# Attention: queries turned in the projection, kept turned in DRAM, and the maxima's row sent through DRAM

## The chip, the cores and the metric

The kernel runs on one core of one Trainium2 chip. The time is device microseconds of one execution, as the median of several runs; a profile is one further execution, recorded by the hardware profiler.

## The reference

One layer of a hybrid backbone. 2048 latent tokens and 256 context tokens of 1024 channels pass one input projection; latent queries (8 heads of 64, 2 key heads) read all latent and context keys in one softmax; a gated branch mixes tokens in chunks of 128; both branches are merged by gates, projected and added, and a feed-forward part with squared ReLU follows. Everything is float32.

```python
q_x = apply_rope(rmsnorm(q_heads(q_x), q_norm_g[l]), cos, sin) * q_scale
k_all = jnp.concatenate([k_c, k_x], axis=2)
v_all = jnp.concatenate([v_c, v_x], axis=2)
s = jnp.einsum('bkgqd,bknd->bkgqn', q, k)      # 2304 keys
p = jax.nn.softmax(s, axis=-1)
o = jnp.einsum('bkgqn,bknd->bkgqd', p, v)
gm_x = gmlp_spatial(gelu(u_x), gelu(vg_x), gm_norm_g[l], gm_ws[l], gm_bs[l])
x = x + g1 * branch_merge(attn_x, gm_x, ga_x, gb_x, ...)
x = x + g2 * sq_relu_mlp(modulate(x, norm2_g[l], sh2, sc2), w_ff1[l], w_ff2[l])
```

## The kernel before, in words

**Precision.** Every float32 product is made of three matmuls on a high part (rounded to the type fp32r by a copy) and a low part (the remainder that a subtraction leaves). So an operand is first *cast* on ScalarE and then its *remainder* is made on VectorE.

**Stages.** Projection and gates run from the start to about 743 us, attention from about 750 to 1430 us, then the merge and the feed-forward part. In the projection (`project`, `tick` L655) the product's matmuls (L1453 to L1455) are written in groups; pieces of side work, written as generators, are advanced by one step at each tick of that list: the query work (`queries_work` L730 to 752), the spatial mixing of the gated branch (L777 on, with its matmuls at L183 to L185 and four slots of the pool `m`), the gates. A `yield` in such a generator puts what follows at a later tick.

**Query work.** For each of 4 blocks of 512 tokens (`TB`; `TT` = 4 tiles of 128 tokens) the queries are loaded in two halves of 4 heads, normalized, turned by the rotary step (`rope` L443, its last instruction L458) and stored token by token in DRAM (`q_d` L218).

**Attention.** A `Unit` (L1850 on) is one block of 512 queries and one pair of heads: 16 units. `attend` (L1084 to L1136) goes through 18 key tiles per unit in 3 groups (gi) of `GROUP` = 6. For each tile, `first` makes the scores by the high queries (L1949) and `second` by the low ones (L1968), ScalarE takes the exponential (L1972), `values` multiplies by the values (L1982), and GpSimd and VectorE sum the probabilities (L1998, L1995, L2011). The scores need each query's maximum beforehand. While a unit runs, TensorE therefore also makes the next unit's scores once in one pass (`maxima`, L1914), which VectorE reduces from PSUM (L1920, L1925); `reference` reduces these to one number per query and head (L1931, with its sign at L1932). The low operand has 128 rows: 64 for a constant and the negative maximum, 64 for the remainder. So the subtraction of the maximum is part of the matmul.

**A unit's queries before.** `load` brings a pair's queries from DRAM, `cast` (L1874) and `remainder` (L1877) split them, `queries` turns the high part by eight transposes (L189, a helper) and two copies (L1889), and `low_queries` does the same with the remainder and the maxima. `load`, `cast` and `remainder` run two units ahead in the first group, `queries` in the second, `reference` one unit ahead in the second group, and `low_queries` at the end of the unit.

**Order.** In attention, TensorE and VectorE follow the order that the source is written in; ScalarE, GpSimd and the queues get theirs from a scheduler. The queue of SP works in order: a transfer that waits holds up the ones behind it. During the first few units VectorE and TensorE also compute part of the modulation vectors (`mod`: L364, L368, the matmuls and L381, L383).

Of the kernel before, what the change touches and what calls it, by code (L numbers as in the profile page):

```python
# [10 lines left out]
F32 = mybir.dt.float32  # L11
F32R = mybir.dt.float32r
# [39 lines left out]
def f32(ap):  # L52
    return ap.bitcast(F32)
# [17 lines left out]
class Kern:  # L71
# [119 lines left out]
    def constants(self):  # L191
# [8 lines left out]
        nc.vector.memset(self.ones, 1.0)  # L200
        self.lead = cp.tile([P, 1], F32, name="lead")
        nc.vector.memset(self.lead, 0.0)
        nc.vector.memset(self.lead[0:1], 1.0)
        self.G1 = cp.tile([P, KC, 2], F32, name="G1")
        self.S1 = cp.tile([P, KC, 2], F32, name="S1")
        self.G2 = cp.tile([P, KC], F32, name="G2")
# [8 lines left out]
        def spill(n, shape):  # L215
            return [dp.tile(shape, F32, tag=f"{n}{b}", name=f"{n}_d{b}") for b in range(NB)]

        self.q_d = spill("q", [TB, NH * HD])  # L218
        self.gm_d = spill("gm", [512, TB])
        self.at_d = spill("at", [512, TB])  # L220
        self.ta_d = spill("ta", [D, TB])
# [508 lines left out]
    def queries_work(self, b):  # L730
        nc = self.nc
        q = [self.m4([TT, 4, HD]) for _ in range(2)]
        flat = [x.rearrange("p t h d -> p t (h d)") for x in q]
        src = self.pr_d[0][b]
        nc.sync.dma_start(flat[0][:, :, :P], self.rows(src[0], slice(2 * P, 3 * P)))
        nc.sync.dma_start(flat[0][:, :, P:], self.rows(src[1], slice(0, P)))
        nc.sync.dma_start(flat[1], self.rows(src[1], slice(P, 3 * P)))
        yield
        yield
        rbs = self.heads_rstd(q, 1.0 / HD)  # L740
        yield
        tabs = self.rope_tables("q", b)
        for c, (raw, rb) in enumerate(zip(q, rbs)):
            nc.vector.tensor_tensor(out=raw, in0=raw, in1=rb, op=ALU.mult)
            yield
            qo = self.m4([TT, 4, HD])
            self.rope(tabs, raw, qo, self.m4([TT, 4, HD]), 4)
            nc.sync.dma_start(
                self.rows(self.q_d[b], slice(c * 256, (c + 1) * 256)),
                qo.rearrange("p t h d -> p t (h d)"),  # L750
            )
            yield

    def raw_values(self, b, j, c):
        x = self.m4([TT, 4, HD])
# [328 lines left out]
    def attend(self, units, late, mod):  # L1084
        self.psum({"b": 8})
        begin = self.here()
        pend = []
        for i, u in enumerate(units):
            at = lambda n: units[n] if 0 <= n < len(units) else None
            nxt, far, old, older = at(i + 1), at(i + 2), at(i - 1), at(i - 2)  # L1090
            for gi, g in enumerate(range(0, NKT, GROUP)):
                group = range(g, g + GROUP)
                step = nxt if gi < 2 else far
                for j in group:
                    u.first(j)
                    u.second(j)
                    if j % GROUP == 2 and far:
                        if gi == 0:
                            far.load()
                        elif gi == 1:  # L1100
                            far.queries()
                    if not nxt:
                        next(late, None)
                    elif i and j % GROUP == 4:
                        next(mod, None)
                if gi == 2 and nxt:
                    nxt.low_queries()
                if step:
                    step.maxima(3)
                for f in pend:  # L1110
                    f()
                if gi == 0 and far:
                    far.cast()
                if gi == 2 and old:
                    old.sums()
                if step:
                    step.maxima(3)
                if gi == 0:
                    if older:
                        older.inverse()  # L1120
                    if far:
                        far.remainder()
                if gi == 1:
                    if nxt:
                        nxt.reference()
                    if old:
                        old.join()
                pend = [lambda u=u, j=j: u.values(j) for j in group]
            pend.append(u.leave)
        for _ in mod:  # L1130
            pass
        for f in pend:
            f()
        units[-2].inverse()
        units[-1].join([self.sb("raw", [TB]) for _ in range(2)])
        self.fixed.append(range(begin, self.here()))  # L1136
# [508 lines left out]
    def build(self):  # L1645
# [27 lines left out]
        def tail(g, p):  # L1673
            u, v = units[0], units[1]
            n = KC - 2
            if (g, p) == (n + 1, 0):
# [1 line left out]
                key_load(0)  # L1678
                u.cast()
                u.remainder()  # L1680
            elif (g, p) == (n, 1):
                u.queries()
            elif (g, p) == (n + 1, 1):
                low_load(0)
            elif (g, p) == (n, 5):
# [1 line left out]
            elif g >= n and p not in (0, 1):  # L1687
                if (g, p) == (n + 1, 5):
# [1 line left out]
                    v.cast()  # L1690
                    v.remainder()
                    value_load((0, 1))
                if (g, p) == (n, 6):
                    v.queries()
                if (g, p) == (n + 1, 6):
                    key_load(1)
                    value_load((2, 3, 4))
# [3 lines left out]
                if (g, p) == (n + 1, 3):  # L1701
                    u.maxima(len(u.todo))
                    u.reference()
                    u.low_queries()
                    v.maxima(6)

        self.project(tail)
# [142 lines left out]
class Unit:  # L1850
# [8 lines left out]

    def load(self):  # L1860
        k, nc = self.k, self.nc
        self.qt = k.t2([TT, 2, HD])
        nc.sync.dma_start(
            self.qt.rearrange("p t h d -> p t (h d)"),
            k.q_d[self.b].rearrange("(t p) c -> p t c", p=P)[
                :, :, self.p * P : (self.p + 1) * P
            ],
        )
        self.pa = k.t4([TT, 2, 2, HD], F32R)
        self.pb = k.t4([TT, 2, P])  # L1870
        nc.gpsimd.memset(self.pb[:, :, :, :HD], 0.0)  # L1871

    def cast(self):
        self.nc.scalar.copy(self.pa, self.qt.unsqueeze(3).broadcast_to([P, TT, 2, 2, HD]))  # L1874

    def remainder(self):
        self.nc.vector.tensor_tensor(  # L1877
            out=self.pb[:, :, :, HD:], in0=self.qt, in1=f32(self.pa[:, :, :, 0, :]),
            op=ALU.subtract,
        )  # L1880

    def turned(self, src):
        k = self.k
        out = []
        for h in range(2):
            ps = k.bank([TB])
            k.transposes(ps, [src(t, h) for t in range(TT)])
            q = k.h2([TB], F32R)
            self.nc.scalar.copy(q, ps)  # L1889
            out.append(q)  # L1890
        return out

    def queries(self):
        self.qa = self.turned(
            lambda t, h: f32(self.pa[:, t, h]).rearrange("p a d -> p (a d)")
        )
        self.mx = self.k.small([TT, 2, NB + 1])

    def maxima(self, n):
        k, nc = self.k, self.nc  # L1900
# [26 lines left out]
                    )  # L1927

    def reference(self):
        nm = self.k.small([TT, 2])  # L1930
        self.nc.vector.tensor_reduce(out=nm, in_=self.mx, axis=AX.X, op=ALU.max)  # L1931
        self.nc.vector.tensor_scalar(  # L1932
            out=self.pb[:, :, :, 0:1], in0=nm.unsqueeze(3), scalar1=-1.0, scalar2=None,
            op0=ALU.mult,
        )

    def low_queries(self):
        self.qb = self.turned(lambda t, h: self.pb[:, t, h, :])

    def keys(self, j):  # L1940
        c, i = (0, j) if j < CTX // P else ((j - 2) // TT + 1, (j - 2) % TT)
# [148 lines left out]
```

## Time and profile before

| | us |
|---|---|
| median of 3 runs | 3111.57 (3110.06 to 3111.89) |
| the profiled execution | 3096.51 |
| its span | 3094.7 |
| TensorE busy in the span | 2991.8 (97%) |
| VectorE busy | 2062.1 (67%) |
| ScalarE busy | 1465.5 (47%) |
| GpSimd busy | 688.6 (22%) |

The profiled execution is 1.8 us longer than its span, which runs from the first to the last instruction. A row of a timeline has start, length, engine, line, operation, output and input, the number of instructions it gathers, and in brackets the idle time before them with its releaser. A row of groups has the busy time, the mean in ns, and the idle time before. PE is TensorE, PEld its weight loads, DVE VectorE, ACT ScalarE, POOL GpSimd, SP the engine whose queue issues most transfers.

### The profile page before, as it was taken

Reading aid. Unit: us, or ns where it says so; the run is one execution under the profiler, and the core shown is the slowest. Engines: PE = TensorE matmul, PEld = TensorE weight load, DVE = VectorE, ACT = ScalarE, POOL = GpSimd, SP = SyncE. Lnnn points to the kernel's source line nnn. Section 1 sums busy time; section 2 is a strip of 40 time slices with the busy share of each in tenths; the row PEclk is TensorE's granted clock in tenths of the full one; section 3 lists DMA queues with packets and bytes.
Section 4 is the critical chain, followed back from the end, with each engine's and each line's share of the span. In section 5 each row is a group of like instructions: output and inputs, shape, how many; then the busy total and the mean of one; then the engine's idle time right before and its main releaser. Section 6 shows DMA issues by size and latency. Waiting matters only on the chain.

```text
span 3094.7 us, 37963 instructions
## 1 busy us (share of the span) xinstructions
PE 2991.8 (97%) x13501; PEld 2253.6 (73%) x13501; DVE 2062.1 (67%) x2918; ACT 1465.5 (47%) x2296; POOL 688.6 (22%) x506
## 2 busy tenths in 40 slices
PE   7999999979999999999999989999999999999999
PEld 4877788866555555556877878887777788888777
DVE  4776577866887777678654488776665566654445
ACT  5646664654554545554222255444454344444433
POOL 0000000002898888885234300000000000000000
PEclk8999999989999999999999999999999999999999
DMA  8686766643110000005855459887766644445665
GB/s 298 204 264 215 233 194 202 195 151 118 38 38 22 14 15 14 5 22 189 277 187 174 141 170 322 308 303 270 252 217 219 207 147 150 152 161 196 205 211 203
DMA packets 385726, 534.32 MB, mean 173 GB/s; under 512 B 32048, under 2 KB 203232, under 8 KB 385536
## 3 DMA queue, kind: packets, MB, share of 16 engines
q1 hardware_dynamic: 375760, 515.88, 50.3%
q10 hardware_dynamic: 9776, 16.01, 1.4%
q8 instruction: 106, 1.74, 0.2%
q14 instruction: 84, 0.69, 0.1%
HBM read 367.69 MB, written 164.10 MB: 172 GB/s over the span
## 4 chain that ended last, share of the span: by engine, by line
PE 78%; DMA 8%; DVE 6%; ACT 4%; issue 3%; POOL 1%; SPq 0%; DVEq 0%; ACTq 0%; POOLq 0%
PE b L1454 13%; PE b L1455 13%; PE b L1453 12%; PE b L1982 8%; PE b L1949 5%; PE b L1968 4%; PE b L1914 3%; PE a L1453 3%; PE b L183 3%; PE b L185 3%; PE a L1455 3%; PE a L1454 3%; PE b L184 3%; PE b L189 2%; DMA bw<-in_w_br_gm 1%
## 5 line engine op out<-in xcount | busy, mean ns | idle before, releaser
L1544 DVE TENSOR_TENSOR b<-b,b 128x1024 fp32r<-128x1024 f32 x224 | 272.9, 1223 | 241.1 <-ACT b L1543 236.3
L1925 DVE TENSOR_REDUCE ts<-b 128x1 f32<-128x512 f32 x512 | 314.7, 681 | 140.9 <-PE b L1914 140.9
L1543 ACT CAST b<-b 128x1024 fp32r<-128x1024 f32 x224 | 234.9, 1052 | 328.2 <-DMA b<-ao_d 290.7
L1454 PE MATMUL b<-b,b 128*128 128x512 f32 x896 | 351.4, 392 | 4.9 <-DVE b L1544 4.2
L1455 PE MATMUL b<-b,b 128*128 128x512 f32 x896 | 349.2, 390 | 0.0
L1453 PE MATMUL b<-b,b 128*128 128x512 f32 x896 | 308.3, 394 | 12.0 <-ACT b L1543 6.4
L1998 POOL TENSOR_TENSOR ac<-ac,p 128x512 f32<-128x512 f32 x216 | 301.5, 1428 | 66.2 <-ACT p L1972 65.4
L1972 ACT ACTIVATE p<-b 128x512 f32<-128x512 f32 x384 | 199.7, 616 | 164.9 <-PE b L1968 155.0
L1998 POOL TENSOR_TENSOR ac<-ac,t 128x512 f32<-128x512 f32 x152 | 217.6, 1456 | 0.0
L1453 PEld LDWEIGHTS b<-b,b 128*128 128x128 f32 x896 | 167.9, 188 | 54.4 <-ACT b L1543 11.3
L1454 PEld LDWEIGHTS b<-b,b 128*128 128x128 f32 x896 | 168.4, 188 | 46.8 <-DVE b L1544 12.4
L1949 PE MATMUL b<-h,h 128*128 128x512 f32 x576 | 199.8, 417 | 1.3 <-ACT p L1972 0.6
L1455 PEld LDWEIGHTS b<-b,b 128*128 128x128 f32 x896 | 168.5, 188 | 34.4
L1968 PE MATMUL b<-h,h 128*128 128x512 f32 x576 | 179.5, 393 | 0.0
L1982 PE MATMUL b<-p,h 128*64 128x512 f32 x768 | 175.3, 598 | 0.0
L1454 PE MATMUL b<-hb,b 128*128 128x512 f32 x448 | 174.6, 390 | 0.0
L1871 POOL MEMSET t<- 128x512 f32 x16 | 8.4, 525 | 696.2 <-DMA tb_d<-t 671.1
L1453 PE MATMUL b<-hb,b 128*128 128x512 f32 x416 | 162.1, 390 | 0.0
L1455 PE MATMUL b<-hb,b 128*128 128x512 f32 x416 | 161.5, 389 | 0.0
L1463 DVE TENSOR_TENSOR f<-f,b 128x512 f32<-128x512 f32 x160 | 109.1, 682 | 65.4 <-issue 43.0
L1949 PEld LDWEIGHTS b<-h,h 128*128 128x128 f32 x576 | 106.2, 189 | 58.5 <-DVE ts L1925 19.4
L1453 PE MATMUL a<-f,h 128*128 128x384 f32 (+1 forms) x320 | 117.5, 372 | 9.9 <-ACT f L607 4.7
(402 smaller groups left out, 6890.5 us busy)
## 6 DMA issues: line engine op xcount, KB each, us to landing
ao_d<-f SPq DMA_DIRECT2D x224, 256.0 KB
b<-ao_d SPq DMA_DIRECT2D x112, 512.0 KB
b<-w2o_d SPq DMA_DIRECT2D x112, 512.0 KB
f<-in_w_ff SPq DMA_DIRECT2D x48, 1024.0 KB
w2o_d<-f SPq DMA_DIRECT2D x112, 256.0 KB
f<-in_w_in SPq DMA_DIRECT2D x44, 512.0 KB
f<-x_d SPq DMA_DIRECT2D x64, 256.0 KB
m<-p_d SPq DMA_DIRECT2D x20, 512.0 KB
```

Of the source, the lines that this page charges most:

```text
L1453: mm(ps, wh, hh, start=start and k == 0, stop=False, skip_group_check=True)
L1454: mm(ps, wh, hl, start=False, stop=False, skip_group_check=True)
L1455: mm(ps, wl, hh, start=False, stop=k == len(w) - 1, skip_group_check=True)
L1463: nc.vector.tensor_tensor(out=out, in0=in0, in1=in1, op=op)
L1543: nc.scalar.copy(h, f32(l))
L1544: nc.vector.tensor_tensor(out=l, in0=f32(l), in1=f32(h), op=ALU.subtract)
L1925: nc.vector.tensor_reduce(out=self.mx[:, t, h, c : c + 1], in_=ps[h], axis=AX.X, op=ALU.max)
L1949: self.nc.tensor.matmul(self.pts[j][h], k.KA[c][self.kv][:, ks], self.qa[h], start=True, stop=False, skip_group_check=True,)
L1968: self.nc.tensor.matmul(s, k.KB[c][self.kv][:, ks], self.qb[h], start=False, stop=True, skip_group_check=True,)
L1972: self.nc.scalar.activation(pt[h], s, AF.Exp)
L1982: nc.tensor.matmul(self.o[h * HD : (h + 1) * HD, :], k.V[c][:, i, self.kv * HD : (self.kv + 1) * HD], pt[h], start=j == 0, stop=j == NKT - 1,)
L1998: nc.gpsimd.tensor_tensor(out=self.acc[e][:, h], in0=old[:, h], in1=pt[h], op=ALU.add)
```

## The change

The queries are turned right behind the rotary step, in the projection: for each half of a block, two groups of four transposes into PSUM, a copy on ScalarE and a store from ScalarE's queue, for each pair of heads one array of 128 channels by 512 tokens in DRAM. Two yields stand ahead of the transposes, and the one behind the store is gone. In attention `load` fetches each head's 64 rows twice, one below the other, in four transfers of rows of 2 KB; `cast` makes the two high tiles and `remainder` the two low ones, both in the second group (cast and remainder were in the first). `reference` reduces the maxima, writes them from 128 partitions by 8 elements into two rows in DRAM, and reads each row back into row 0 of a low tile, over the remainder's duplicate that stood there. The constant row that meets it (`lead`) is -1 instead of 1, so the multiplication by -1 is gone. `queries`, `low_queries`, `turned` and the memset of GpSimd are gone.

```diff
--- before.py
+++ after.py
@@ -200,7 +200,7 @@
         nc.vector.memset(self.ones, 1.0)
         self.lead = cp.tile([P, 1], F32, name="lead")
         nc.vector.memset(self.lead, 0.0)
-        nc.vector.memset(self.lead[0:1], 1.0)
+        nc.vector.memset(self.lead[0:1], -1.0)
         self.G1 = cp.tile([P, KC, 2], F32, name="G1")
         self.S1 = cp.tile([P, KC, 2], F32, name="S1")
         self.G2 = cp.tile([P, KC], F32, name="G2")
@@ -215,7 +215,13 @@
         def spill(n, shape):
             return [dp.tile(shape, F32, tag=f"{n}{b}", name=f"{n}_d{b}") for b in range(NB)]
 
-        self.q_d = spill("q", [TB, NH * HD])
+        self.q_d = [
+            [dp.tile([P, TB], F32, tag=f"q{b}_{p}", name=f"q_d{b}_{p}") for p in range(NH // 2)]
+            for b in range(NB)
+        ]
+        self.mx_d = [
+            dp.tile([2, TB], F32, tag=f"mx{u}", name=f"mx_d{u}") for u in range(NB * NH // 2)
+        ]
         self.gm_d = spill("gm", [512, TB])
         self.at_d = spill("at", [512, TB])
         self.ta_d = spill("ta", [D, TB])
@@ -745,11 +751,20 @@
             yield
             qo = self.m4([TT, 4, HD])
             self.rope(tabs, raw, qo, self.m4([TT, 4, HD]), 4)
-            nc.sync.dma_start(
-                self.rows(self.q_d[b], slice(c * 256, (c + 1) * 256)),
-                qo.rearrange("p t h d -> p t (h d)"),
-            )
-            yield
+            yield
+            yield
+            for f in range(2):
+                ps = self.bank([TB])
+                self.transposes(
+                    ps,
+                    [
+                        qo[:, t, 2 * f : 2 * f + 2].rearrange("p h d -> p (h d)")
+                        for t in range(TT)
+                    ],
+                )
+                ot = self.t2([TB])
+                nc.scalar.copy(ot, ps)
+                nc.scalar.dma_start(self.q_d[b][2 * c + f], ot)
 
     def raw_values(self, b, j, c):
         x = self.m4([TT, 4, HD])
@@ -1094,22 +1109,17 @@
                 for j in group:
                     u.first(j)
                     u.second(j)
-                    if j % GROUP == 2 and far:
-                        if gi == 0:
-                            far.load()
-                        elif gi == 1:
-                            far.queries()
+                    if j % GROUP == 2 and far and gi == 0:
+                        far.load()
                     if not nxt:
                         next(late, None)
                     elif i and j % GROUP == 4:
                         next(mod, None)
-                if gi == 2 and nxt:
-                    nxt.low_queries()
                 if step:
                     step.maxima(3)
                 for f in pend:
                     f()
-                if gi == 0 and far:
+                if gi == 1 and far:
                     far.cast()
                 if gi == 2 and old:
                     old.sums()
@@ -1118,9 +1128,9 @@
                 if gi == 0:
                     if older:
                         older.inverse()
+                if gi == 1:
                     if far:
                         far.remainder()
-                if gi == 1:
                     if nxt:
                         nxt.reference()
                     if old:
@@ -1678,8 +1688,6 @@
                 key_load(0)
                 u.cast()
                 u.remainder()
-            elif (g, p) == (n, 1):
-                u.queries()
             elif (g, p) == (n + 1, 1):
                 low_load(0)
             elif (g, p) == (n, 5):
@@ -1690,8 +1698,6 @@
                     v.cast()
                     v.remainder()
                     value_load((0, 1))
-                if (g, p) == (n, 6):
-                    v.queries()
                 if (g, p) == (n + 1, 6):
                     key_load(1)
                     value_load((2, 3, 4))
@@ -1701,7 +1707,6 @@
                 if (g, p) == (n + 1, 3):
                     u.maxima(len(u.todo))
                     u.reference()
-                    u.low_queries()
                     v.maxima(6)
 
         self.project(tail)
@@ -1859,42 +1864,22 @@
 
     def load(self):
         k, nc = self.k, self.nc
-        self.qt = k.t2([TT, 2, HD])
-        nc.sync.dma_start(
-            self.qt.rearrange("p t h d -> p t (h d)"),
-            k.q_d[self.b].rearrange("(t p) c -> p t c", p=P)[
-                :, :, self.p * P : (self.p + 1) * P
-            ],
-        )
-        self.pa = k.t4([TT, 2, 2, HD], F32R)
-        self.pb = k.t4([TT, 2, P])
-        nc.gpsimd.memset(self.pb[:, :, :, :HD], 0.0)
+        self.raw = [k.t2([TB]) for _ in range(2)]
+        for h, raw in enumerate(self.raw):
+            src = k.q_d[self.b][self.p][h * HD : (h + 1) * HD]
+            for i in range(2):
+                nc.sync.dma_start(raw[i * HD : (i + 1) * HD], src)
 
     def cast(self):
-        self.nc.scalar.copy(self.pa, self.qt.unsqueeze(3).broadcast_to([P, TT, 2, 2, HD]))
+        self.qa = [self.k.h2([TB], F32R) for _ in range(2)]
+        for q, raw in zip(self.qa, self.raw):
+            self.nc.scalar.copy(q, raw)
+        self.mx = self.k.small([TT, 2, NB + 1])
 
     def remainder(self):
-        self.nc.vector.tensor_tensor(
-            out=self.pb[:, :, :, HD:], in0=self.qt, in1=f32(self.pa[:, :, :, 0, :]),
-            op=ALU.subtract,
-        )
-
-    def turned(self, src):
-        k = self.k
-        out = []
-        for h in range(2):
-            ps = k.bank([TB])
-            k.transposes(ps, [src(t, h) for t in range(TT)])
-            q = k.h2([TB], F32R)
-            self.nc.scalar.copy(q, ps)
-            out.append(q)
-        return out
-
-    def queries(self):
-        self.qa = self.turned(
-            lambda t, h: f32(self.pa[:, t, h]).rearrange("p a d -> p (a d)")
-        )
-        self.mx = self.k.small([TT, 2, NB + 1])
+        self.qb = [self.k.h2([TB], F32R) for _ in range(2)]
+        for q, hi, raw in zip(self.qb, self.qa, self.raw):
+            self.nc.vector.tensor_tensor(out=q, in0=raw, in1=f32(hi), op=ALU.subtract)
 
     def maxima(self, n):
         k, nc = self.k, self.nc
@@ -1927,15 +1912,15 @@
                     )
 
     def reference(self):
-        nm = self.k.small([TT, 2])
-        self.nc.vector.tensor_reduce(out=nm, in_=self.mx, axis=AX.X, op=ALU.max)
-        self.nc.vector.tensor_scalar(
-            out=self.pb[:, :, :, 0:1], in0=nm.unsqueeze(3), scalar1=-1.0, scalar2=None,
-            op0=ALU.mult,
-        )
-
-    def low_queries(self):
-        self.qb = self.turned(lambda t, h: self.pb[:, t, h, :])
+        k, nc = self.k, self.nc
+        nm = k.small([2, TT])
+        nc.vector.tensor_reduce(
+            out=nm.rearrange("p h t -> p t h"), in_=self.mx, axis=AX.X, op=ALU.max
+        )
+        row = k.mx_d[self.b * (NH // 2) + self.p]
+        nc.sync.dma_start(row.rearrange("h (t p) -> p h t", p=P), nm)
+        for h in range(2):
+            nc.sync.dma_start(f32(self.qb[h])[0:1], row[h : h + 1])
 
     def keys(self, j):
         c, i = (0, j) if j < CTX // P else ((j - 2) // TT + 1, (j - 2) % TT)
```

## The prediction

> **What bounds the kernel now.** I read first the head of the page, then its chain of work that ended last, then the windows of the stages that the diff touches, and only then single lines.
>
> ```profile
> span 3094.7 us, 37963 instructions
> PE 2991.8 (97%) x13501; PEld 2253.6 (73%) x13501; DVE 2062.1 (67%) x2918; ACT 1465.5 (47%) x2296; POOL 688.6 (22%) x506
> PE 78%; DMA 8%; DVE 6%; ACT 4%; issue 3%; POOL 1%; SPq 0%; DVEq 0%; ACTq 0%; POOLq 0%
> ...
> 800.00:900.00 100.00, 100.00 (x482) 55.78 (x480) 87.17 (x110) 52.10 (x101) 86.35 (x62) 1.00 0.12 38
> 1000.00:1100.00 100.00, 99.99 (x474) 54.76 (x472) 69.13 (x100) 52.05 (x100) 84.05 (x65) 1.00 0.03 11
> ```
>
> The last two lines are windows inside attention (PE, PEld, DVE, ACT, POOL busy, clock, DMA share). TensorE is without a gap there at the full clock, so every matmul that leaves attention is time, as long as no other engine steps into its place. VectorE is near: 87% where it also computes the modulation (window 800 to 900), 69% where it does not. ScalarE at 52% and the DMA engines at 3 to 12% have room; GpSimd, at 84 to 86%, keeps its own work except a memset. The profiled execution took 3096.51 us, 1.8 us more than its span and 0.5% below the median of 3111.57. I make the sum against 3096.5 and move the result up by the 15 us between the two.
>
> **Transposes out of attention.** Each of 16 units turned its query tiles twice, eight transposes each time. The prologue's two units do so before attention, but PE is as dense there.
>
> ```profile
> L189 PE MATMUL b<-ident,t 128*128 128x128 f32 x296 | 38.3, 273 | 0.0
> ...
> 807.33 1.03 PE L189 MATMUL b<-ident,t 128*128 128x128 f32 x8
> 808.12 0.71 PE L1949 MATMUL b<-h,h 128*128 128x512 f32 x2
> ...
> 824.28 1.04 PE L189 MATMUL b<-ident,t 128*128 128x128 f32 x8
> 825.24 1.40 PE L1914 MATMUL b<-h,h 64*128 64x256 f32 x10
> ```
>
> The group's mean of 273 ns is one instruction's own length in a pipeline; what eight cost is read from starts. The first set takes 808.12 − 807.33 = 0.79 us. The second takes 825.24 − 824.28 = 0.96 us, of which I leave half of the 0.17 difference to the change of matmul shape behind it, and count 0.88. 16 × (0.79 + 0.88) = 26.7 us go. The Trainium skill (TensorE: Matmul & The Clock Gate, Part 4: PE-mode transpose) gives about 275 ns for one in a kernel's context; by that, taken as a rate, 256 would be worth an estimated 70 us, and the starts above say that here it is a length and not a rate.
>
> **Transposes into the projection.** 64 transposes, in 16 groups of four, are added. Groups of that kind already stand there:
>
> ```profile
> 658.59 0.62 PE L189 MATMUL b<-ident,m 128*128 128x128 f32 x4
> 658.97 0.48 PE L1454 MATMUL a<-h,f 128*128 128x512 f32 x1
> ...
> 659.51 0.60 PE L189 MATMUL b<-ident,m 128*128 128x128 f32 x4
> 659.87 0.48 PE L1454 MATMUL a<-h,f 128*128 128x512 f32 x1
> ```
>
> 0.38 and 0.36 us by the starts: 16 × 0.37 = +5.9 us.
>
> The order of the changed program puts all 16 of block 0's transposes (both halves) just ahead of the product's matmul that ran at 197.18. Their input is the rotary step on VectorE:
>
> ```profile
> 196.83 1.22 DVE L458 TENSOR_TENSOR m<-m,m 128x1024 f32<-128x1024 f32 x1
> ...
> 201.44 1.22 DVE L458 TENSOR_TENSOR m<-m,m 128x1024 f32<-128x1024 f32 x1
> ...
> 197.18 0.39 PE L1453 MATMUL a<-f,h 128*128 128x512 f32 x1
> ```
>
> The halves end at about 198.0 and 202.7. TensorE, in order, waits 0.8 us, turns eight, and waits some 3.8 more; behind it stands the whole product. I count 4.4 us, with 2 to 6: a dip of the clock may follow, and a later wait may absorb some. For blocks 1 to 3 the transposes stand behind the end of their rotary steps, so I count no wait; if that cover went, each would cost as block 0.
>
> The two extra yields per half move later work of the projection back by ticks. What that does to its end is the least certain term. There TensorE already waits:
>
> ```profile
> 656.58 0.39 PE L183 MATMUL b<-m,m 128*128 128x256 f32 x1 [1.29 <-DMA m<-ws_d]
> ...
> 669.46 0.80 PE L1453 MATMUL a<-hx,e 128*128 128x512 f32 x1 [5.44 <-DVE t L1835]
> ...
> 686.80 0.55 PE L183 MATMUL b<-m,m 128*128 128x256 f32 x1 [4.91 <-DMA m<-ws_d]
> ```
>
> The last spatial mixing (L183) hangs on a chain through four slots, one turn of which takes 30.2 us by these rows (656.58 to 686.80). In the new order it enters TensorE 9 to 16 matmul groups later, and the last chain starts some 4 to 5 us later, while about 7 us of gate work on VectorE no longer lies ahead of it. I count +3, with −3 to +7. The query stores change from the SP queue to eight pairs on ScalarE's, and one 128x512 copy on ScalarE comes with each; nothing waits for them before attention.
>
> **The casts and remainders.** ScalarE loses two 128x512 copies and half of the wide cast per unit, which frees it; nothing waited for it.
>
> ```profile
> L1889 ACT CAST h<-b 128x512 fp32r<-128x512 f32 x64 | 36.6, 662 | 0.0
> ...
> L1877 DVE TENSOR_TENSOR t<-t,t x16: 691/1649/1676, 697.2 to 1322.9; 128x512 f32<-128x512 f32 x16
> ...
> L1932 DVE TENSOR_SCALAR t<-ts x16: 175/946/962, 742.4 to 1377.9; 128x8 f32<-128x8 f32 x16
> ```
>
> VectorE gets two remainders of 1.65 us where it had one, and loses 0.95: +2.4 us per unit, and the 3.3 now lie in the second third of the unit, right ahead of the reference. That 1.65 is the price under GpSimd's traffic; undisturbed, the same form takes 0.69. The Trainium skill (SBUF — State Buffer, Who interferes with whom) has an instruction with two SBUF inputs wait for GpSimd's reads; the two durations agree with that. Who waits for VectorE there? TensorE, for the PSUM banks of the maxima. Cover is VectorE's own idle time:
>
> ```profile
> 876.63 3.68 DVE L1925 TENSOR_REDUCE ts<-b 128x1 f32<-128x512 f32 x6 [1.39 <-PE b L1914]
> ...
> 919.40 3.68 DVE L1925 TENSOR_REDUCE ts<-b 128x1 f32<-128x512 f32 x6 [0.47 <-PE b L1914]
> ...
> 1040.76 2.48 DVE L1920 TENSOR_REDUCE ts<-b 128x2 f32<-128x512 f32 x4 [1.86 <-PE b L1914]
> ...
> 1048.24 3.08 DVE L1925 TENSOR_REDUCE ts<-b 128x1 f32<-128x512 f32 x5 [2.19 <-PE b L1914]
> ```
>
> In an ordinary unit 1.86 + 2.19 = 4.05 us are free against the 3.3 needed: nothing. In the four units with modulation work the idle gaps between bursts of maxima sum to about 1.7, 1.9, 0.5 and 1.9 us (the first two rows show such gaps), and what is missing makes TensorE wait by my account 2.0, 1.1, 3.2 and 1.1: +7 us, with 0 to 9, as free banks and later gaps can absorb it.
>
> **The maxima's row.** The reference went through eight transposes. Now 1024 elements of 4 bytes go to DRAM, and two rows of 2 KB come back into the query tile, from SP's queue. Behind the waiting write on SP stand the two reads, and in two or three units a load of modulation weights; who waits is the next unit's first score matmul.
>
> ```profile
> 1036.59 0.20 DVE L1931 TENSOR_REDUCE ts<-ts 128x8 f32<-128x40 f32 x1
> ...
> 1049.32 0.63 PE L1968 MATMUL b<-h,h 128*128 128x512 f32 x2
> ...
> 1064.16 0.36 SPq L1863 DMA_DIRECT2D t<-q_d  x1
> ...
> 1065.00:1065.50 0.50, 0.50 (x6) 0.44 (x5) 0.50 (x2) 0.50 (x2) 0.50 (x2) 1.00 0.21 56
> 1065.50:1066.00 0.50, 0.50 (x7) 0.50 (x6) 0.50 (x2) 0.50 (x2) 0.50 (x1) 1.00 1.02 306
> ...
> 1134.00 0.53 ACTq L2033 DMA_DIRECT2D sm_d<-t  x2
> ...
> 1135.51 0.32 SPq L2042 DMA_DIRECT2D t<-sm_d  x1
> ```
>
> From the end of the reduce (1036.79) to the matmul are 12.5 us; less 1.0 as transposes vanish and 3.3 for the remainders now ahead, 8.2 are left. No row shows a 4-byte write to DRAM. The nearest is the old query load, 512 pieces of 512 bytes: issued at 1064.16, first packets a microsecond later, and at 306 GB/s an engine-packet takes 16 × 512 / 306 = 27 ns. At that price 1024 pieces take 1.7 us, at twice that 3.4. A small write is visible to its reader within 1.0 us of its issue ending (1134.53 to 1135.51). Write: 1.0 + 1.7 to 3.4 + up to 0.5; the reads: 0.7 to issue, 1.0 to start, 0.6 to land. 5.5 to 7.2 us, and I take 6.2: in time, by 2 us. If a piece costs three times, 3.7 us more than my low end, the row is 1 us late. The Trainium skill (DMA: Bandwidth & Descriptors, Specifications) says that transfers below 512 bytes are done as read-modify-write, and elsewhere on that page that a DMA has some 2 us fixed. By two fixed costs and a doubled packet that is an estimated 7.4 us, still in time; no run here shows that write.
>
> **The sum.** −26.7 + 5.9 + 4.4 + 3 + 7 = −6.4 us: 3090 for a profiled execution, 3105 on the median. With the small ends of the stalls (2, −3, 0) it is −22; with the large ones (6, 7, 9) +1.
>
> **Rivals.**
>
> *The row is late (slower).* It decides from a trip of about 8.2 us; each microsecond beyond costs TensorE that microsecond in up to 15 units (the first is covered by the prologue). A trip of 10.5 us gives 15 × 2.3 = +35: 3140. For it: a 4-byte write is unmeasured, the margin is 2 us, and VectorE's lateness eats the same margin. Against it: DMA engines 3 to 12% busy, and the prices above. 24%.
>
> *VectorE becomes the bound in attention (slower).* If the two remainders displace maxima in ordinary units too, 11 more units lose their 3.3 us less half their gaps, about 1.5 each: +16, 3121. For it: 1.65 us apiece, and TensorE's period shrinks by 1.7 us. Against it: 69% busy at 1000 to 1100. 7%.
>
> *The stalls are hidden (faster).* Banks and gaps absorb VectorE's lateness, the end of the projection does not move, block 0 waits for 3 us: −26.7 + 5.9 + 3 = −18, 3094. 23%.
>
> *The end of the projection breaks open (about as before).* A further turn of slots waits for the shifted ticks, +6 beyond my 3: 3111. 6%.
>
> That the transposes do not leave is excluded by the order of the changed program: 256 leave the attention's part and 64 enter.
>
> **How the numbers follow.** The forecast case has 40%, its own range 3092 to 3112. A change under 0.2%, 6.2 us, can hardly be told from none. Faster by more: half of the forecast case, all of the hidden stalls, a little of the others, 0.46. Within: most of the other half and the open end of the projection, 0.23. Slower: 0.31, from the late row and VectorE. The range reaches from 3091 to 3142; what is left out is mainly a row later than 2.5 us.
>
> **What would show it.** Right: no L189 on query tiles in attention, L1949 to L1968 without a gap at unit starts, a wait of 4 to 5 us on L458 near 197 us, attention shorter by 15 to 20 us. Wrong: a gap at each unit's first score matmul released by a DMA (late row); gaps of the maxima's matmuls released by L1925 in all units (VectorE); a span of the projection that grows by more than 15 us.

## The result and the profile after

The changed kernel takes 3157.45 us (median of 4 runs, 3150.0 to 3160.55) against 3110.82 us for the kernel before. The ratio is 1.0166, with a 95% interval of 1.015 to 1.0182: slower by 1.7%, outside the range that was given. The profiled execution took 3150.0 us.

The head of the page of the changed kernel, its chain, one group of matmuls, and the window over all of attention:

```profile
span 3148.2 us, 37685 instructions
PE 2992.9 (95%) x13309; PEld 2249.8 (71%) x13309; DVE 2064.0 (66%) x2918; ACT 1446.0 (46%) x2264; POOL 684.7 (22%) x490
PE 72%; DMA 13%; DVE 8%; ACT 4%; issue 2%; POOL 1%; SPq 0%; ACTq 0%; DVEq 0%; POOLq 0%
...
L1953 PE MATMUL b<-h,h 128*128 128x512 f32 x576 | 196.7, 425 | 38.2 <-DMA h<-mx_d 38.2
...
768.00:1486.00 718.00, 673.98 (x2952) 366.21 (x2952) 509.02 (x676) 328.03 (x640) 579.95 (x408) 0.95 0.11 30
```

TensorE is no longer without a gap in attention: 674 us busy of 718, at a mean clock of 0.95. One group has all of a new wait: the first score matmul with the low queries (L1953, L1968 before) waits 38.2 us for the maxima's row from DRAM. DMA in the chain grew from 8% to 13%.

The same place in the timelines of SP and of TensorE, at one unit's end:

```profile
1029.38 0.39 SPq L1921 DMA_DIRECT2D mx_d<-ts  x1
1037.90 0.52 SPq L1923 DMA_DIRECT2D h<-mx_d  x2
...
1037.72 0.88 PE L1934 MATMUL b<-h,h 128*128 128x512 f32 x2
1041.54 0.91 PE L1953 MATMUL b<-h,h 128*128 128x512 f32 x2 [2.94 <-DMA h<-mx_d]
```

The write is issued at 1029.38, and the first read, which waits until the write is confirmed (counts as done), only at 1037.90. The pieces themselves were through soon. The view of DMA over 1029.4 to 1037.9 has 1040 packets, all small: the 1024 pieces and 16 more. The windows show where: they move in the one from 1030 to 1031 us (DMA share 0.47), 1.6 us after the issue at the latest, and none in the next (0.00).

```profile
DMA packets 1040, 0.00 MB, mean 0 GB/s; under 512 B 1040, under 2 KB 1040, under 8 KB 1040
...
1030.00:1031.00 1.00, 1.00 (x8) 0.45 (x6) 1.00 (x1) 0.68 (x2) 1.00 (x2) 1.00 0.47 4
1031.00:1032.00 1.00, 1.00 (x6) 0.29 (x4) 1.00 (x3) 0.00 (x0) 1.00 (x1) 1.00 0.00 0
...
1041.00:1042.00 1.00, 0.46 (x2) 0.23 (x2) 0.04 (x1) 0.00 (x0) 0.00 (x0) 1.00 0.73 227
1042.00:1043.00 1.00, 1.00 (x6) 0.83 (x6) 0.00 (x0) 0.86 (x2) 0.00 (x0) 1.00 0.42 141
1043.00:1044.00 1.00, 1.00 (x4) 0.81 (x3) 0.00 (x0) 0.98 (x3) 0.08 (x1) 0.52 0.01 4
1044.00:1045.00 1.00, 1.00 (x3) 0.78 (x3) 0.00 (x0) 0.39 (x2) 1.00 (x1) 0.50 0.00 0
1045.00:1046.00 1.00, 1.00 (x4) 0.74 (x3) 0.00 (x0) 1.00 (x2) 1.00 (x2) 0.50 0.00 0
1046.00:1047.00 1.00, 1.00 (x5) 0.82 (x4) 0.00 (x0) 0.44 (x2) 0.43 (x1) 0.77 0.02 8
```

The later rows show a second price. After the wait the clock is granted at half for about 3 us (0.52, 0.50, 0.50, 0.77), while TensorE is busy in every one of them. The Trainium skill (TensorE: Matmul & The Clock Gate, Part 1: The HAM clock gate) puts the fall to half rate at some 3.4 us of idleness; here a gap of 2.94 us was followed by it, and one of 0.87 us at another unit was not: there the clock stayed at 1.00. Over all 16 waits the trace has half clock at or right behind the 14 of 1.4 us and longer, for 3.4 or 6.8 us mostly, and none at the two of 0.87 and 0.76 us. So in this kernel less idleness than the page's was enough, and the measurement decides; yet in e3 below a gap of 1.99 us had no half clock behind it, so the length of the gap alone doesn't settle it.

Unit by unit, from the first score matmul of each third (us):

| | first third | second | last | unit |
|---|---|---|---|---|
| before, ninth unit | 13.62 | 13.78 | 15.37 | 42.8 |
| after, ninth unit | 17.57 | 12.80 | 14.39 | 44.8 |
| row by contiguous write (e2), ninth unit | 13.61 | 12.80 | 14.40 | 40.8 |

The two sets of transposes are gone from the second and last third, 0.98 us each. The wait and the slow clock behind it add 4.0 us to the first. Attention, from the first score matmul to the end of the last value matmul, went from 676.6 to 717.4 us. It starts 18 us later as well:

```profile
L1949 PE MATMUL b<-h,h x576: 387/390/800, 750.8 to 1415.3; 128*128 128x512 f32 x192
```

```profile
L1934 PE MATMUL b<-h,h x576: 387/390/799, 768.8 to 1474.0; 128*128 128x512 f32 x192
```

(These are the first score matmuls before and after; the columns behind the lengths are the first and last start.) Of the 53.5 us by which the span grew, 18.0 lie ahead of attention and 40.7 in it, and 5.2 are won behind it. What follows attention took 1667.3 us before and 1662.1 after; in the runs below it scatters from 1667 to 1682 with no edit there, so that single profiles are compared by stage and kernels by medians.

### The profile page after: what moved, and what is told of

Its sections match the earlier page's. It is cut to its first block, busy times and chain, and to the rows that moved or that the text cites. A ratio compares the mean times of both kernels' runs of the same rounds, so it can differ in the third digit from the quotient of the medians.

```text
span 3148.2 us, 37685 instructions
## 1 busy us (share of the span) xinstructions
PE 2992.9 (95%) x13309; PEld 2249.8 (71%) x13309; DVE 2064.0 (66%) x2918; ACT 1446.0 (46%) x2264; POOL 684.7 (22%) x490
## 4 chain that ended last, share of the span: by engine, by line
PE 72%; DMA 13%; DVE 8%; ACT 4%; issue 2%; POOL 1%; SPq 0%; ACTq 0%; DVEq 0%; POOLq 0%
PE b L1464 13%; PE b L1465 13%; PE b L1463 13%; PE b L1967 6%; DMA mx_d<-ts 5%; PE b L1953 3%; PE b L183 3%; PE b L185 3%; PE b L184 3%; PE b L1934 3%; PE a L1463 3%; PE a L1464 3%; PE a L1465 3%; PE b L1899 2%; DVE ts L1910 2%
## 5 line engine op out<-in xcount | busy, mean ns | idle before, releaser
L1463 PE MATMUL b<-b,b 128*128 128x512 f32 x896 | 308.3, 394 | 12.6 <-ACT b L1553 6.9
L1953 PE MATMUL b<-h,h 128*128 128x512 f32 x576 | 196.7, 425 | 38.2 <-DMA h<-mx_d 38.2
L1983 POOL TENSOR_TENSOR ac<-p,p 128x512 f32<-128x512 f32 x32 | 40.9, 1300 | 820.7 <-ACT p L1957 820.7
L1934 PE MATMUL b<-h,h 128*128 128x512 f32 x576 | 207.4, 436 | 3.9 <-DVE ts L1910 3.3
L1953 PEld LDWEIGHTS b<-h,h 128*128 128x128 f32 x576 | 117.7, 205 | 69.4 <-DMA h<-mx_d 44.6
L1934 PEld LDWEIGHTS b<-h,h 128*128 128x128 f32 x576 | 116.3, 204 | 59.5 <-DVE ts L1910 16.8
```

The costliest lines, as they stand in the source:

```text
L1463: mm(ps, wh, hh, start=start and k == 0, stop=False, skip_group_check=True)
L1934: self.nc.tensor.matmul(self.pts[j][h], k.KA[c][self.kv][:, ks], self.qa[h], start=True, stop=False, skip_group_check=True,)
L1953: self.nc.tensor.matmul(s, k.KB[c][self.kv][:, ks], self.qb[h], start=False, stop=True, skip_group_check=True,)
L1983: nc.gpsimd.tensor_tensor(out=self.acc[e][:, h], in0=old[:, h], in1=pt[h], op=ALU.add)
```

## The experiments

The main theory was that the write is confirmed late and that everything else is about as forecast. Rivals: that small pieces are slow anywhere, that a trip through DRAM is slow at any number of pieces, that VectorE starts the trip too late.

**e1: the row without DRAM.**

```diff
-        nc.sync.dma_start(row.rearrange("h (t p) -> p h t", p=P), nm)
-        for h in range(2):
-            nc.sync.dma_start(f32(self.qb[h])[0:1], row[h : h + 1])
+        for h in range(2):
+            for t in range(TT):
+                nc.sync.dma_start(f32(self.qb[h])[0:1, t * P : (t + 1) * P], nm[:, h, t : t + 1])
```

> The maxima go from their 128 partitions straight into row 0 of the low tiles, in eight transfers of 128 elements of 4 bytes, without DRAM. The main theory (the write to DRAM is confirmed some 8 us late, and the reads stand behind it) expects the row in time: no wait for it ahead of the first score matmuls, the first third of a unit back at 13.6 us, 3090 to 3105 us. A rival, that small pieces are slow wherever they go, expects the wait to stay: 3140 to 3160.

3103.68 us; ratio to the kernel before 0.9972 (0.9957 to 0.9987). No wait for the row is left, and ordinary units take 40.8 us. So 1024 pieces of 4 bytes are not slow in every place: eight transfers of 128 pieces, issued over 5 us, were all in time. (That 1024 in one write to DRAM needn't be slow either, e9 shows below.)

**e2: the write in 128 pieces of 32 bytes.** The row is stored as the partitions hold it; the reads collect it.

```diff
-            dp.tile([2, TB], F32, tag=f"mx{u}", name=f"mx_d{u}") ...
+            dp.tile([P, 2 * TT], F32, tag=f"mx{u}", name=f"mx_d{u}") ...
-        nc.sync.dma_start(row.rearrange("h (t p) -> p h t", p=P), nm)
+        nc.sync.dma_start(row, nm.rearrange("p h t -> p (h t)"))
...
-            nc.sync.dma_start(f32(self.qb[h])[0:1], row[h : h + 1])
+            nc.sync.dma_start(
+                f32(self.qb[h])[0:1].rearrange("o (t p) -> o t p", p=P),
+                row[:, h * TT : (h + 1) * TT].rearrange("p t -> t p").unsqueeze(0),
+            )
```

> The write to DRAM is made of 128 pieces of 32 bytes in place of 1024 of 4; the two reads collect 512 elements of 4 bytes each. If the late confirmation is paid per piece (main theory), the write takes 2 to 3 us and the trip some 6: no wait, 3090 to 3110. If it is a fixed price of a write to DRAM that is read back, the write keeps its 8.5 us and the time stays at 3150 to 3160, or more by slower reads.

3102.54 us; 0.9975 (0.9962 to 0.9987). SP's timeline of this kernel at one unit, and the window over its attention:

```profile
1098.29 0.32 SPq L1922 DMA_DIRECT2D mx_d<-ts  x1
1099.72 1.96 SPq L1924 DMA_DIRECT2D h<-mx_d  x2
...
773.00:1431.00 658.00, 651.08 (x2952) 348.38 (x2952) 518.38 (x675) 326.35 (x640) 585.18 (x408) 0.99 0.13 32
```

The read is issued 1.43 us after the write, in place of 8.5. So a trip through DRAM isn't slow whatever the pieces. Attention takes 657.5 us here against 717.4: the late row cost 60 us. 38.2 of the change's are waits for it. Most of the rest is the half clock behind them: TensorE is busy for 674 us in the change and for 651 here, with the same number of matmuls.

**e3: cast and remainder in the first third,** the row as in the change.

```diff
-                if gi == 1 and far:
+                if gi == 0 and far:
                     far.cast()
...
                     if older:
                         older.inverse()
+                    if far:
+                        far.remainder()
                 if gi == 1:
-                    if far:
-                        far.remainder()
                     if nxt:
                         nxt.reference()
```

> Cast and remainder go back to the first third of a unit, so that the reduce that makes the row starts about 3.3 us earlier; the trip through DRAM stays. If the wait of 2.3 to 2.9 us is a matter of when the trip starts, it vanishes or falls below 0.5 us, and the time falls to 3100 to 3115. If the lateness is VectorE's in general, the maxima of the first third run late in its place and the time stays above 3140.

3131.18 us; 1.0069 (1.0047 to 1.0091), between the two expectations. TensorE's waits for the row (us in total, times, longest):

```profile
PE b L1953 <- DMA h<-mx_d: 22.7, 16, 3.4
```

The waits fell from 38.2 to 22.7 us but did not go. From the end of the reduce to the first use it is now 12.6 to 13.4 us in the ordinary units, against 11.5 to 12.2 in the change: the trip took more of the time that it was given, and the earlier start bought only some 1.5 us a unit. Why the trip grew isn't shown. When it starts is part of the matter, but e2, which starts it where the change does, has next to no wait: its length decides.

**e4: no row.** The maxima are reduced but not subtracted, and the exponential takes its input times 0.001.

```diff
-        row = k.mx_d[self.b * (NH // 2) + self.p]
-        nc.sync.dma_start(row.rearrange("h (t p) -> p h t", p=P), nm)
-        for h in range(2):
-            nc.sync.dma_start(f32(self.qb[h])[0:1], row[h : h + 1])
...
-            self.nc.scalar.activation(pt[h], s, AF.Exp)
+            self.nc.scalar.activation(pt[h], s, AF.Exp, scale=1e-3)
```

> The row is left out altogether: the maxima are reduced but not subtracted, and the exponential takes the scores times 0.001. All theories expect no wait for the row; it shows what the other edits come to: attention shorter than before by 16 to 30 us, its start 18 us later, 3095 to 3105 in all. If the time stays above 3120, the cost isn't the row's.

3105.59 us; 0.9989 (0.9977 to 1.0002). Attention takes 656.7 us, within 1 us of e2's. So e2 has hidden the row in full; in e1 attention is 3 us longer (659.8).

**e9, e10, e11: what makes the confirmation late.** All three write 1024 pieces of 4 bytes; only the places in DRAM differ, and with them the reads, which now collect single elements.

```diff
-            dp.tile([2, TB], F32, tag=f"mx{u}", name=f"mx_d{u}") ...
+            dp.tile([2, TB, 16], F32, tag=f"mx{u}", name=f"mx_d{u}") ...    # e10: [2, TB, 4]
-        row = k.mx_d[self.b * (NH // 2) + self.p]
+        row = k.mx_d[self.b * (NH // 2) + self.p][:, :, 0]
```

```diff
+            dp.tile([P, 64], F32, tag=f"mx{u}", name=f"mx_d{u}") ...        # e11
+        row = k.mx_d[...][:, :16].rearrange("p (e z) -> p e z", z=2)[:, :, 0]
+        nc.sync.dma_start(row, nm.rearrange("p h t -> p (h t)"))
...      # the reads collect as in e2
```

> The changed kernel with each of the 1024 elements of the maxima written to a 64-byte line of its own in DRAM; the reads collect 512 elements each. If the late confirmation goes by the number of pieces, the write keeps 8.5 to 11 us, and the time is 3150 to 3165. If it comes from many small writes into the same line, one after another, the write falls to 2 to 4 us, the row is in time, and the time is 3098 to 3108.

> The changed kernel with the 1024 elements of the maxima 16 bytes apart in DRAM: four to a 64-byte line, over 16 KB. Before, 16 to a line over 4 KB took 8.5 to 11 us until the reads were issued, one to a line over 64 KB took 2.4 to 3.2 (4.2 in two units with other loads between). If writes into one line are done one after another, the write takes about (9.8 - 2.7) x 3/15 + 2.7 = 4 us; if it is enough that neighbours don't touch, 2.7.

> 1024 pieces of 4 bytes again, eight of one partition into one 64-byte line, the lines 256 bytes apart, so over 32 KB. If lines that many pieces share are the cause, the write takes about half of the changed kernel's, 5 to 6 us; if it was the small region of 4 KB, it falls to about 2.7 as with one piece to a line; if sharing only hurts between pieces of different partitions, it falls too.

SP's timelines of e9, of e10 and of e11, each the write and the reads behind it:

```profile
1053.63 0.39 SPq L1922 DMA_DIRECT2D mx_d<-ts  x1
1056.19 1.19 SPq L1924 DMA_DIRECT2D h<-mx_d  x2
```

```profile
1094.47 0.36 SPq L1922 DMA_DIRECT2D mx_d<-ts  x1
1097.69 1.19 SPq L1924 DMA_DIRECT2D h<-mx_d  x2
```

```profile
1124.79 0.36 SPq L1923 DMA_DIRECT2D mx_d<-ts  x1
1129.89 1.70 SPq L1925 DMA_DIRECT2D h<-mx_d  x2
```

Medians over the seventh to fifteenth unit, from the end of the reduce to the issue of the first read:

| pieces of 4 bytes | to 64 bytes | region | us |
|---|---|---|---|
| the change, next to each other | 16 | 4 KB | 9.8 (8.6 to 10.8) |
| e11, 8 bytes apart, groups 256 bytes apart | 8 | 32 KB | 5.2 (4.9 to 5.5) |
| e10, 16 bytes apart | 4 | 16 KB | 3.2 (2.8 to 3.7) |
| e9, 64 bytes apart | 1 | 64 KB | 2.7 (2.5 to 3.2) |
| e2, 128 pieces of 32 bytes | – | 4 KB | 1.5 |

The number of pieces is the same in four of these kernels, and the time follows how many of them share a short stretch of DRAM, by about 0.6 us for each further piece between 8 and 16 (4.6 / 8); below that the steps are small, and the spans of e10 and e9 overlap. In all four the packets had passed 1.6 us after the issue. The region's size does not order them: 16 KB is faster than 32 KB. Nor would stretches of 128 bytes or more, where e10 would share as many as or more than e11; stretches of 64 and of 32 bytes fit alike, and but for the 0.5 us between e10 and e9 those of 16 bytes too. That the pieces are done one after another in a stretch is the reading that fits; the traces don't show it directly. The Trainium skill (DMA: Bandwidth & Descriptors, Specifications) has transfers below 512 bytes as read-modify-write; such an order would fit that, but the page doesn't speak of neighbours in one stretch. It can't be the whole reason: e2's pieces of 32 bytes are far below 512 too, and its reads could follow after 1.5 us.

e9 took 3098.52 us, 0.9963 (0.9949 to 0.9976), with nothing but the stride changed. e10 gave 3099.04 us in one run and e11 3169.77 us in one run, where the kernel before gave 3117.12 beside them. So e11 is about as far above the kernel before as the change is (1.7%), although its write is quicker. In the seventh to fifteenth unit the row was used 11.0 to 11.9 us after the reduce, 5 to 6 us behind the issue of its second read, where the change's reads of contiguous 2 KB took 1.0 to 3.4. I had not counted that: 512 elements of 4 bytes can cost the reader as much as they save the writer. e2 reads in the same manner, and its write is early enough. The waits for the row in e11, and the one that is left in e2, where the second row came 6.2 us behind its read's issue (columns: us in total, times, longest):

```profile
PE b L1958 <- DMA h<-mx_d: 36.1, 29, 2.9
```

```profile
PE b L1957 <- DMA h<-mx_d: 0.3, 1, 0.3
```

**e5: e2 and e3's edit together.**

> The write of 128 pieces of 32 bytes together with cast and remainder in the first third of a unit. With the row in time, units with modulation work still take 44.9 and 43.6 us where ordinary ones take 40.8. If it is the place of the remainders, ahead of the reduce, that makes VectorE late there, they fall by 1 to 3 us each and the time by 3 to 7, to 3095 to 3100. If it is VectorE's load as a whole, they stay and the time stays at 3100 to 3105.

3096.59 us; 0.9957 (0.9944 to 0.997). The gain is not in the units meant: the four with modulation work take 44.2, 41.4, 44.2 and 41.4 us, 171.2 together, against 42.1, 44.9, 41.7 and 43.6, 172.3 together, in e2. The profile's difference is that attention starts at 767 in place of 773 us, by one and the same code of the projection. The place of the remainders is not what makes these units long. That start scatters by as much between e6 and e8 below, whose projection is the same too, so what gave the 6 us in the medians is open.

**e6 and e7: the ticks of the projection.** e6 is e2 with the transposes of a half at the next step that is there anyway; e7 is the kernel before with one more yield per half.

```diff
         for c, (raw, rb) in enumerate(zip(q, rbs)):            # e6
             nc.vector.tensor_tensor(out=raw, in0=raw, in1=rb, op=ALU.mult)
+            if c:
+                turn(0, qo)
             yield
             qo = self.m4([TT, 4, HD])
             self.rope(tabs, raw, qo, self.m4([TT, 4, HD]), 4)
             yield
-            yield
-            for f in range(2): ...
+        turn(1, qo)             # the same transposes, copy and store
```

```diff
                 qo.rearrange("p t h d -> p t (h d)"),          # e7
             )
             yield
+            yield
```

> The write of 128 pieces of 32 bytes, and the transposes in the projection without extra yields: those of a half run at the next step that is there anyway, so that all later work keeps its tick. Attention began at 769 to 773 us where the kernel before began at 751. If the shifted ticks make the 7 us wait for a gate's product and the 10 us wait for the mixing's weights at its end, these go back to about 5 each and attention begins at 755 to 762, 3088 to 3096 us in all. If the transposes with their copies and buffers do it, it begins at 767 or later and the time stays at 3100 to 3105.

> The kernel before with one more yield per half in the query work and nothing else. If the shift of ticks alone costs the end of the projection some 8 to 12 us, attention begins at 758 to 763 and the time is 3118 to 3124. If it costs nothing, both stay at 751 and 3111.

e6: 3092.4 us; 0.9947 (0.9931 to 0.9963). e7: 3112.19 us; 1.0008 (0.9998 to 1.0018), in its median not to be told from no change, where 3118 to 3124 were expected if the shift alone costs. The waits of TensorE at the end of the projection, in the changed kernel, in e7 and in e6:

```profile
691.87 0.79 PE L1463 MATMUL a<-hx,t 128*128 128x512 f32 x1 [7.21 <-ACT a L1846]
706.25 0.55 PE L183 MATMUL b<-m,m 128*128 128x256 f32 x1 [9.98 <-DMA m<-ws_d]
```

```profile
678.59 0.80 PE L1454 MATMUL a<-hx,t 128*128 128x512 f32 x1 [7.87 <-ACT a L1842]
691.66 0.55 PE L183 MATMUL b<-m,m 128*128 128x256 f32 x1 [7.74 <-DMA m<-ws_d]
```

```profile
693.99 0.80 PE L1468 MATMUL a<-hx,t 128*128 128x512 f32 x1 [5.08 <-ACT a L1851]
698.53 0.39 PE L183 MATMUL b<-m,m 128*128 128x256 f32 x1 [0.78 <-DMA m<-ws_d]
```

With the shifted ticks the two waits are 17.2 us, with the shift alone 15.6, without it 5.9. Attention starts at 758.7 us in e6 and at 755.5 in e7. So the shift of ticks makes these two waits long, and the transposes at unshifted ticks don't. What that is worth in time is less sure. Attention starts at 767 to 774 us in the nine profiles that have both the shift and the transposes, and at 756 to 765 in the three that have the transposes alone (e6, e8, e12). But the shift alone started it only 4.7 us later than before, and left the median where it was.

**e8: e2, e3's edit and e6's together.**

> The three edits together: the write of 128 pieces of 32 bytes, cast and remainder in the first third, and transposes in the projection without extra yields. If their gains add, attention begins at 756 to 760 us, lasts 655 to 658, and the time is 3086 to 3092 us, against 3092.4 without the early remainder and 3096.6 without the tick-neutral transposes. If the early remainder's 6 us were only the scatter of the projection's end (767 against 773 us for one and the same code), it adds nothing: 3091 to 3095.

3097.07 us; 0.9957 (0.9941 to 0.9973). That is above both expectations. The gains don't add: attention lasts 658.2 us, as without the early remainder, and starts at 764.6, later than in e6. Why it starts later with the same projection is open. Against e5 the unshifted ticks won nothing in the median (3096.59 there), against e2 they won 10 us.

**e12: e6, with block 0's second half turned later.** Its transposes are a piece of side work behind the one that is drained with it.

```diff
-        turn(1, qo)
+        if b:
+            turn(1, qo)
+        else:
+            self.work.insert(2, self.turn_later(turn, qo))
```

> The write of 128 pieces of 32 bytes and the tick-neutral transposes; in addition, the second half of block 0 is turned only after the piece of side work that is drained together with it, so that TensorE need not wait 3.6 us for the rotary step there. If that wait is time, and not slack that is waited for elsewhere, the time falls by 3 to 4 us against 3092.4, to 3088 to 3090. If other waits take its place, it stays at 3090 to 3095.

3091.34 us; 0.9941 (0.9924 to 0.9958). The wait of 3.6 us for the rotary step is gone from the trace, and attention starts at 755.7, but the median is only 1 us below e6's, well inside their scatter. e6 and e12 are the fastest versions, 0.5 to 0.6% under the kernel before.

## Why the prediction was wrong

**The step that failed** is the price of the maxima's write. I took the per-packet time of the old query load, 27 ns of an engine, for pieces of 4 bytes and added 1.5 us for start and end: 3.2 to 4.9 us. The pieces had passed 1.6 us after the issue, quicker than that. But it took 8.6 to 11.1 us until the reads could be issued, and e9 to e11 show that this goes with the 16 pieces that share each 64 bytes. The row I leaned on was a load from DRAM, in pieces of 512 bytes, and the write that I took for small had rows of 2 KB; neither has pieces that share a short stretch. The factor of up to two that I allowed was too small, and it was in the wrong place, on the packet and not on its confirmation.

**The rival was the right one, with 24%.** Its place, the first score matmul of each unit, and its releaser, a DMA, are what the trace shows. The time available was near: 9.1 us in e2 against 8.2 forecast. Its price was too low. I had a trip of 10.5 us and only the wait; the trip was 11.5 to 12.9, and 14 of the 16 waits had half clock behind them, so that the row cost 60 us and not 35. (In the prediction's case of a piece at three times the price the slip is small: two further times 1.7 are 3.4 us and not 3.7.)

**Transposes out:** 0.98 + 0.97 us per unit against 0.79 + 0.88; 31 us against 26.7. To read them from starts and not from the group's mean of 273 ns was right.

**Into the projection:** the wait in block 0 is in the trace as forecast:

```profile
200.22 1.09 PE L189 MATMUL b<-ident,m 128*128 128x128 f32 x8 [0.62 <-DVE m L464]
204.92 1.30 PE L189 MATMUL b<-ident,m 128*128 128x128 f32 x5 [3.61 <-DVE m L464]
```

4.2 us against 4.4. (The two gaps that the prediction reads, 0.8 and 3.8, would make 4.6.) Its "two extra yields per half" are one: two were added and one taken away. The projection's end was undersized in the trace: the two waits there, 7.5 us before, became 17.2. Attention started 18 us later where the terms gave 13, and that although the prologue lost 24 transposes. In the medians +3 was forecast; e2 against e6 shows 10 and e5 against e8 nothing, so its size is not settled.

**VectorE in the units with modulation work:** +7 forecast. In e2 these four are 9.1 us longer than four ordinary units, before they were 1.2: +8. The size was right. The reason was right in part. TensorE does wait for VectorE there, four times in e2's trace, 3.8 us in all; but the place of the remainders ahead of the reference isn't why, for e5 moved them and the sum stayed. Where the rest of the 8 us comes from isn't shown. The "+2.4 us per unit" for VectorE was a slip: two remainders for one remainder and the sign are 3.3 − 1.65 − 0.95 = +0.7 by the prediction's rows, and in e2's ordinary units they take 2.8 us where 2.6 were before. The four waits, by the gaps that it gives, would be 1.6, 1.4, 2.8 and 1.4: about the same sum. (ScalarE was relieved by more than the prediction has, four copies and the wide cast a unit for two casts; nothing waited for it.)

**The rest of the sum held.** With the row in time the same edits gave 3098.5 to 3103.7 us (e1, e2, e9), where the sum gave 3105. That is partly luck, since terms that were off cancel: the transposes were worth 4 us more than forecast, and attention started 5 us later. The rival of hidden stalls (3094) did not come, and VectorE did not become the bound in ordinary units: their second and last thirds shrank by what the transposes had taken.

## What to carry to other kernels

Where a small array goes through DRAM to change its layout, write it in the order in which the partitions hold it, or spread the elements, and let the reader collect if there are some 6 us for that; 1024 single elements beside each other cost 8.6 to 11 us until a dependent read started, and 1.5 us as 128 runs of 32 bytes. A wait in front of a dense stretch of matmuls can cost more than its length: with 14 of the 16 waits here came half clock, for 3.4 us or more. And an extra yield in side work isn't sure to be free: with it two waits at the projection's end grew from 7.5 to 15.6 us, though by itself that didn't show in the median.

## What was not expected of the hardware

The time until a DMA write counts as done went with the number of pieces that fall into the same 64 bytes or less: 9.8, 5.2, 3.2 and 2.7 us for 16, 8, 4 and 1, while the packets of each had passed 1.6 us after the issue. With reads of 512 single elements into one row it took 5 to 6 us from the second read's issue to the first use (e11), with reads of contiguous 2 KB 1.0 to 3.4; why isn't shown. And the change's waits of TensorE of 1.4 to 4.2 us all came with a half clock.
